# Average pooling 2x2: the multiply by 0.25 moved from ScalarE to VectorE, and the last tile split in 16, 8, 8

## The chip, the cores and the metric

The kernel runs on one core of a Trainium2 chip. The metric is device time in microseconds (us), as a median of several executions; lower is better. The profile shows the "span" of one execution, about 1.8 us shorter than its device time.

## The reference

```python
# x: float32 [32, 128, 256, 256], kernel_size = 2, stride = 2
for i in range(h_out):
    for j in range(w_out):
        window = x[:, :, 2*i:2*i+2, 2*j:2*j+2]
        output[:, :, i, j] = np.mean(window, axis=(2, 3))
```

1073.7 MB are read and 268.4 MB are written: each output is the sum of four inputs, times 0.25.

## The kernel before

An output row and its two input rows are one "row" of work; 128 rows, one per partition, are one unit, and there are 4096 units. A tile is 32 units: 64 KB of input and 16 KB of output per partition, 8.39 MB and 2.10 MB in all. There are 127 whole tiles (0 to 126) and a last one that is split in parts. Two input buffers and two result buffers alternate (a third result buffer serves the last tile alone). SyncE issues the loads, VectorE adds, ScalarE multiplies and issues the stores.

```python
    def sums(it, dst):                       # VectorE
        dve.tensor_add(out=it[:, :, 0:w], in0=it[:, :, 0:w], in1=it[:, :, w:]).then_inc(halfway)
        take(dve, halfway)                   # take = wait for a semaphore, then count it down
        dve.tensor_add(out=dst, in0=it[:, :, 0:w:2], in1=it[:, :, 1:w:2]).then_inc(summed)

    def tile_sums(b):
        take(dve, stored[b], 16)             # the store of two tiles ago has landed
        take(dve, loaded[b], 16)             # the load has landed
        sums(ins[b], res[b])

    def scale_store(t, b, landed):           # ScalarE
        take(act, summed)
        act.sem_inc(free[b])                 # SyncE may issue the load of tile t + 2
        scale(res[b])                        # act.mul(..., mul=0.25)
        take(act, scaled)
        act.dma_start(out=ot[t], in_=res[b]).then_inc(landed, 16)
    # ... SyncE: wait for free[b], load(t, b); then the parts of the last tile
    # ... parts of the last tile: 16, 8, 4, 4 units
    # ... the store of tile 126 is issued by SyncE, the parts' stores by ScalarE
```

Of the kernel before, what the change touches and what calls it, by code (L numbers as in the profile page):

```python
# [9 lines left out]
@with_exitstack  # L10
def kernel(
    ctx: ExitStack,
    tc: tile.TileContext,
    x: bass.AP,
    kernel_size: bass.AP,
    stride: bass.AP,
    out: bass.AP,
):
    nc = tc.nc
    P = nc.NUM_PARTITIONS  # L20

    n, c, h, w = x.shape
    k = int(kernel_size)
    s = int(stride)
    h_out = (h - k) // s + 1
    w_out = (w - k) // s + 1
    R = n * c * h_out
    units = R // P if R % P == 0 else 0


    if k == 2 and s == 2 and h % 2 == 0 and w == 256 and units >= 1024:
        _pool_2x2(ctx, tc, x, out, units)
    else:
        _generic_pool(ctx, tc, x, out, k, s, n, c, h, w, h_out, w_out)
# [5 lines left out]
def _pool_2x2(ctx, tc, x, out, units):  # L40
    nc = tc.nc
    P = nc.NUM_PARTITIONS
    f32 = mybir.dt.float32
    w = x.shape[3]
    w_out = w // 2
    sp, act, dve = nc.sync, nc.scalar, nc.vector

    xv = x.rearrange("n c (ho a) w -> (n c ho) (a w)", a=2)
    ov = out.rearrange("n c ho wo -> (n c ho) wo")


    in_pool = ctx.enter_context(tc.tile_pool(name="inp", bufs=2))
    out_pool = ctx.enter_context(tc.tile_pool(name="outp", bufs=3))
    ins = [in_pool.tile([P, TILE, 2 * w], f32, name="in_tile") for _ in range(2)]
    res = [out_pool.tile([P, TILE, w_out], f32, name="res") for _ in range(3)]

    def sem(name):
        return ctx.enter_context(nc.semaphore(name))

    loaded, free, stored = [[sem(f"{n}{b}") for b in range(2)] for n in ("loaded", "free", "stored")]  # L60
    halfway, summed, scaled, held, tail = [sem(n) for n in ("halfway", "summed", "scaled", "held", "tail")]



    def take(engine, sem, n=1):
        engine.wait_ge(sem, n)
        engine.sem_inc(sem, -n)  # L67

    def block(r0, g):
        rows = slice(r0, r0 + g * P)  # L70
        return xv[rows].rearrange("(p g) f -> p g f", p=P), ov[rows].rearrange("(p g) f -> p g f", p=P)

    whole, rest = divmod(units - 1, TILE)
    rest += 1
    xt = xv[0:whole * TILE * P].rearrange("(t p g) f -> t p g f", p=P, g=TILE)
    ot = ov[0:whole * TILE * P].rearrange("(t p g) f -> t p g f", p=P, g=TILE)
    parts, a = [], 0
    while a < rest:
        b = rest if rest - a <= 4 else a + (rest - a) // 2
        parts.append((a, b, sem(f"part{len(parts)}")))  # L80
        a = b

    def load(t, b):
        sp.dma_start(out=ins[b], in_=xt[t]).then_inc(loaded[b], 16)

    def sums(it, dst):
        dve.tensor_add(out=it[:, :, 0:w], in0=it[:, :, 0:w], in1=it[:, :, w:]).then_inc(halfway)  # L87
        take(dve, halfway)
        dve.tensor_add(out=dst, in0=it[:, :, 0:w:2], in1=it[:, :, 1:w:2]).then_inc(summed)  # L89

    def tile_sums(b):
        take(dve, stored[b], 16)
        take(dve, loaded[b], 16)
        sums(ins[b], res[b])

    def scale(dst, done=scaled):
        act.mul(out=dst, in_=dst, mul=0.25).then_inc(done)  # L97

    def scale_store(t, b, landed):
        take(act, summed)  # L100
        act.sem_inc(free[b])
        scale(res[b])
        take(act, scaled)
        act.dma_start(out=ot[t], in_=res[b]).then_inc(landed, 16)

    with tc.tile_critical():

        load(0, 0)
        load(1, 1)
        pairs = (whole - 2) // 2  # L110
        with sp.Fori(2, 2 + 2 * pairs, 2) as i:
            for b in range(2):
                take(sp, free[b])
                load(i + b, b)
        for t in range(2 + 2 * pairs, whole):
            take(sp, free[t % 2])
            load(t, t % 2)



        take(sp, free[whole % 2])
        it, dst = ins[whole % 2], res[2]
        for a, b, part in parts:
            sp.dma_start(out=it[:, a:b], in_=block((whole * TILE + a) * P, b - a)[0]).then_inc(part, 16)
        take(sp, held)
        sp.dma_start(out=ot[whole - 1], in_=res[(whole - 1) % 2]).then_inc(tail, 16)


        for b in range(2):
            dve.sem_inc(stored[b], 16)  # L130
        with dve.Fori(0, whole // 2):
            for b in range(2):
                tile_sums(b)
        if whole % 2:
            tile_sums(0)
        for a, b, part in parts:
            take(dve, part, 16)
            sums(it[:, a:b], dst[:, a:b])


        scale_store(0, 0, stored[0])
        pairs = (whole - 3) // 2
        with act.Fori(1, 1 + 2 * pairs, 2) as i:
            for b in (1, 0):
                scale_store(i + 1 - b, b, stored[b])
        for t in range(1 + 2 * pairs, whole - 1):
            scale_store(t, t % 2, stored[t % 2] if t < whole - 2 else tail)
        take(act, summed)
        scale(res[(whole - 1) % 2], held)
        for a, b, _ in parts:  # L150
            take(act, summed)
            scale(dst[:, a:b])
            take(act, scaled)
            act.dma_start(out=block((whole * TILE + a) * P, b - a)[1], in_=dst[:, a:b]).then_inc(tail, 16)


        take(sp, tail, 16 * (len(parts) + 2))
# [95 lines left out]
```

## Time and profile before

| | before |
|---|---|
| device time, median of 3 | 3103.32 us |
| VectorE busy / ScalarE busy | 54% / 15% |
| data moved, mean rate | 1342.2 MB, 433 GB/s |
| time from one tile to the next | 24.19 us |

From the page of the kernel before: the span, the busy time of each engine, the DMA row (each digit is the busy share of one fortieth of the span, in tenths), and the two DMA queues, q1 of the loads and q10 of the stores, with their share of the 16 DMA engines' time.

```profile
span 3101.5 us, 2614 instructions
DVE 1679.6 (54%) x262; ACT 464.7 (15%) x132; POOL 0.2 (0%) x4
...
DMA  9999999999999999999999999999999999999999
...
DMA packets 37728, 1342.19 MB, mean 433 GB/s; under 512 B 4192, under 2 KB 4192, under 8 KB 4576
...
q1 hardware_dynamic: 19008, 1075.85, 80.1%
q10 hardware_dynamic: 18720, 266.35, 20.1%
```

The two queues' shares add up to all of the engines' time: the DMA engines are full until shortly before the end, and nothing else is. The Trainium skill, "SBUF — State Buffer", section "SBUF: two separate sides", gives about 436 GB/s as what the DMA side of SBUF can carry; this trace agrees with 433.

The timeline of the kernel before in mid-run (start, duration, engine, line, operation; in brackets the idle time of the engine before it and what ended it):

```profile
1012.79 8.69 DVE L87 TENSOR_TENSOR in_tile<-in_tile 128x8192 f32<-128x8192 f32 x1 [10.93 <-DVEq L67]
1021.63 4.42 DVE L89 TENSOR_TENSOR res<-in_tile 128x4096 f32<-128x4096 f32 x1
1026.24 3.62 ACT L97 ACTIVATE res<-res 128x4096 f32<-128x4096 f32 x1 [20.58 <-ACTq L67]
1030.09 0.34 ACTq L104 DMA_DIRECT2D out_dram<-res  x1
1037.01 8.69 DVE L87 TENSOR_TENSOR in_tile<-in_tile 128x8192 f32<-128x8192 f32 x1 [10.95 <-DVEq L67]
```

VectorE waits 10.9 us in each tile. L67 is the wait for a semaphore; both a store's and a load's landing are waited for there. The DMA issues of the same kernel (count, size where known, median us from issue to landing):

```profile
out_dram<-res ACTq DMA_DIRECT2D x126, 2048.0 KB, 30.8
...
in_tile<-in_x_dram SPq DMA_DIRECT2D x127, 31.5
```

With a tile starting at T, its store is issued at T+17.3 and lands near T+48.1, just ahead of the start of the tile that uses the same buffers, at T+48.4. The load for that tile was issued at T+13.6 and landed near T+45.1. So in the kernel before VectorE is released by the store of two tiles ago; the load has been there for 3.27 us (median over the tiles, from the trace's landing records).

The end of the kernel before:

```profile
3067.57 8.69 DVE L87 TENSOR_TENSOR in_tile<-in_tile 128x8192 f32<-128x8192 f32 x1 [9.71 <-DVEq L67]
3076.41 4.43 DVE L89 TENSOR_TENSOR res<-in_tile 128x4096 f32<-128x4096 f32 x1
3080.75 4.42 DVE L87 TENSOR_TENSOR in_tile<-in_tile 128x4096 f32<-128x4096 f32 x1
...
3094.44 0.69 DVE L89 TENSOR_TENSOR res<-in_tile 128x512 f32<-128x512 f32 x1
3095.25 0.63 ACT L97 ACTIVATE res<-res 128x512 f32<-128x512 f32 x1 [1.34 <-ACTq L67]
3095.98 0.34 ACTq L154 DMA_DIRECT2D out_dram<-res  x1
```

Only here does VectorE work without a gap: from the start of tile 126 at 3067.57 its chain leads to the last store at 3095.98. That store in the DMA issues of the last microseconds, with its time to landing:

```profile
out_dram<-res ACTq DMA_DIRECT2D x1, 256.0 KB, 4.4
```

### The profile page before, as it was taken

To read this page: it belongs to the slowest core of one execution; us is meant where nothing else is said; L and a number is where in the kernel's file an instruction comes from. 1 tells how busy PE (TensorE), PEld (TensorE's weight loads), DVE (VectorE), ACT (ScalarE), POOL (GpSimd) and SP (SyncE) were. 2 spreads that over 40 slices of the span, in tenths; PEclk is the share of its full clock that TensorE was granted. 3 is DMA by queue.
4 is the path that set the end of the run, shared out by engine and by line. 5 is a ranking of instruction groups with operands and counts; after the bars stand their busy time and mean duration, and the time that the engine had idled before them with its cause. 6 is when DMAs were issued, how large, how long until landed. Compare 5 with 4: busy or idle time off the path is not lost. (4 is left out here: it accounts for less than half of the span.)

```text
span 3101.5 us, 2614 instructions
## 1 busy us (share of the span) xinstructions
DVE 1679.6 (54%) x262; ACT 464.7 (15%) x132; POOL 0.2 (0%) x4
## 2 busy tenths in 40 slices
DVE  4555555555555555555555555555555555555556
ACT  1111111111111111111111111111111111111111
POOL 0000000000000000000000000000000000000000
DMA  9999999999999999999999999999999999999999
GB/s 416 436 440 426 436 440 426 437 440 424 438 440 423 439 437 425 440 428 434 440 433 430 442 423 436 439 427 440 435 426 437 439 427 436 438 424 439 437 425 416
DMA packets 37728, 1342.19 MB, mean 433 GB/s; under 512 B 4192, under 2 KB 4192, under 8 KB 4576
## 3 DMA queue, kind: packets, MB, share of 16 engines
q1 hardware_dynamic: 19008, 1075.85, 80.1%
q10 hardware_dynamic: 18720, 266.35, 20.1%
HBM read 1073.74 MB, written 268.44 MB: 433 GB/s over the span
## 5 line engine op out<-in xcount | busy, mean ns | idle before, releaser
L87 DVE TENSOR_TENSOR in_tile<-in_tile 128x8192 f32<-128x8192 f32 (+1 forms) x131 | 1113.0, 8496 | 1396.4 <-DVEq L67 1396.4
L97 ACT ACTIVATE res<-res 128x4096 f32<-128x4096 f32 (+1 forms) x131 | 463.5, 3538 | 2594.8 <-ACTq L67 2594.8
L89 DVE TENSOR_TENSOR res<-in_tile 128x4096 f32<-128x4096 f32 (+1 forms) x131 | 566.8, 4327 | 19.2
L97 ACT ACT_TABLE_LOAD x1 | 1.3, 1283 | 36.3 <-ACTq L67 36.3
L234 POOL MEMSET const-bfloat16-1.0<- 128x1 bf16 x1 | 0.1, 101 | 0.0
L234 POOL MEMSET const-uint8-127<- 128x1 uint8 x1 | 0.1, 101 | 0.0
L234 POOL MEMSET const-float32-0.0<- 128x1 f32 x1 | 0.1, 98 | 0.2 <-issue 0.2
L234 POOL MEMSET const-float32-1.0<- 128x1 f32 x1 | 0.1, 98 | 0.0
## 6 DMA issues: line engine op xcount, KB each, us to landing
out_dram<-res ACTq DMA_DIRECT2D x126, 2048.0 KB, 30.8
in_tile<-in_x_dram SPq DMA_DIRECT2D x1, 4096.0 KB, 22.0
in_tile<-in_x_dram SPq DMA_DIRECT2D x1, 2048.0 KB, 27.1
in_tile<-in_x_dram SPq DMA_DIRECT2D x2, 1024.0 KB, 30.0
out_dram<-res SPq DMA_DIRECT2D x1, 2048.0 KB, 11.7
in_tile<-in_x_dram SPq DMA_DIRECT2D x127, 31.5
out_dram<-res ACTq DMA_DIRECT2D x1, 1024.0 KB, 8.1
out_dram<-res ACTq DMA_DIRECT2D x1, 512.0 KB, 6.0
```

The costliest lines, as they stand in the source:

```text
L87: dve.tensor_add(out=it[:, :, 0:w], in0=it[:, :, 0:w], in1=it[:, :, w:]).then_inc(halfway)
L89: dve.tensor_add(out=dst, in0=it[:, :, 0:w:2], in1=it[:, :, 1:w:2]).then_inc(summed)
L97: act.mul(out=dst, in_=dst, mul=0.25).then_inc(done)
L234: nc = _bacc.Bacc("TRN2", target_bir_lowering=False, num_devices=1)
```

## The change

The intent: let VectorE, which is idle 46% of the time, do the scaling in place, so that a tile has one hop between engines less before its store, and use fewer parts at the end. The diff, without renamings and loops, and without tile 126, whose store now waits for VectorE's multiply instead of ScalarE's:

```diff
-        b = rest if rest - a <= 4 else a + (rest - a) // 2      # 16, 8, 4, 4
+        b = rest if rest - a <= 8 else a + (rest - a) // 2      # 16, 8, 8
 ...
-        dve.tensor_add(out=dst, in0=it[:, :, 0:w:2], in1=it[:, :, 1:w:2]).then_inc(summed)
+        dve.tensor_add(out=dst, in0=it[:, :, 0:w:2], in1=it[:, :, 1:w:2]).then_inc(halfway)
+        take(dve, halfway)
+        dve.tensor_scalar_mul(out=dst, in0=dst, scalar1=0.25).then_inc(done)
 ...
-    def scale_store(t, b, landed):
-        take(act, summed)
+    def store(t, b, landed):
+        take(act, ready)
         act.sem_inc(free[b])
-        scale(res[b])
-        take(act, scaled)
         act.dma_start(out=ot[t], in_=res[b]).then_inc(landed, 16)
 ...
         for a, b, _ in parts:
-            take(act, summed)
-            scale(dst[:, a:b])
-            take(act, scaled)
+            take(act, ready)
             act.dma_start(...)
```

One side effect: the slot (the tile's input buffer) is now freed after the multiply, not before it, so the next load is issued later in the tile.

More of the change, by code (lines that the diff above doesn't have):

```diff
@@ L60, in _pool_2x2 @@
     loaded, free, stored = [[sem(f"{n}{b}") for b in range(2)] for n in ("loaded", "free", "stored")]
-    halfway, summed, scaled, held, tail = [sem(n) for n in ("halfway", "summed", "scaled", "held", "tail")]
+    halfway, ready, held, tail = [sem(n) for n in ("halfway", "ready", "held", "tail")]
     def take(engine, sem, n=1):
@@ L84, in load, with means, tile_means @@
         sp.dma_start(out=ins[b], in_=xt[t]).then_inc(loaded[b], 16)
-    def sums(it, dst):
+    def means(it, dst, done):
         dve.tensor_add(out=it[:, :, 0:w], in0=it[:, :, 0:w], in1=it[:, :, w:]).then_inc(halfway)
         take(dve, halfway)
-        dve.tensor_add(out=dst, in0=it[:, :, 0:w:2], in1=it[:, :, 1:w:2]).then_inc(summed)
-    def tile_sums(b):
+        dve.tensor_add(out=dst, in0=it[:, :, 0:w:2], in1=it[:, :, 1:w:2]).then_inc(halfway)
+        take(dve, halfway)
+        dve.tensor_scalar_mul(out=dst, in0=dst, scalar1=0.25).then_inc(done)
+    def tile_means(b, done):
         take(dve, stored[b], 16)
         take(dve, loaded[b], 16)
-        sums(ins[b], res[b])
-    def scale(dst, done=scaled):
-        act.mul(out=dst, in_=dst, mul=0.25).then_inc(done)
-    def scale_store(t, b, landed):
-        take(act, summed)
+        means(ins[b], res[b], done)
+    def store(t, b, landed):
+        take(act, ready)
         act.sem_inc(free[b])
-        scale(res[b])
-        take(act, scaled)
         act.dma_start(out=ot[t], in_=res[b]).then_inc(landed, 16)
@@ L130, in _pool_2x2 @@
             dve.sem_inc(stored[b], 16)
-        with dve.Fori(0, whole // 2):
+        pairs = (whole - 1) // 2
+        with dve.Fori(0, pairs):
             for b in range(2):
-                tile_sums(b)
-        if whole % 2:
-            tile_sums(0)
+                tile_means(b, ready)
+        for t in range(2 * pairs, whole):
+            tile_means(t % 2, ready if t < whole - 1 else held)
         for a, b, part in parts:
             take(dve, part, 16)
-            sums(it[:, a:b], dst[:, a:b])
-        scale_store(0, 0, stored[0])
-        pairs = (whole - 3) // 2
-        with act.Fori(1, 1 + 2 * pairs, 2) as i:
-            for b in (1, 0):
-                scale_store(i + 1 - b, b, stored[b])
-        for t in range(1 + 2 * pairs, whole - 1):
-            scale_store(t, t % 2, stored[t % 2] if t < whole - 2 else tail)
-        take(act, summed)
-        scale(res[(whole - 1) % 2], held)
+            means(it[:, a:b], dst[:, a:b], ready)
+        pairs = (whole - 2) // 2
+        with act.Fori(0, 2 * pairs, 2) as i:
+            for b in range(2):
+                store(i + b, b, stored[b])
+        for t in range(2 * pairs, whole - 1):
+            store(t, t % 2, stored[t % 2] if t < whole - 2 else tail)
         for a, b, _ in parts:
-            take(act, summed)
-            scale(dst[:, a:b])
-            take(act, scaled)
+            take(act, ready)
             act.dma_start(out=block((whole * TILE + a) * P, b - a)[1], in_=dst[:, a:b]).then_inc(tail, 16)
```

## The prediction

> **What bounds it now.** Data movement. The page's first table has VectorE busy 54% and ScalarE 15% of 3101.5 us, while the DMA row is at nine tenths or more in all 40 slices and moves 433 GB/s. 1342.2 MB at that rate is the whole span. The Trainium skill, "SBUF — State Buffer", section "SBUF: two separate sides", gives the DMA side of SBUF ~436 GB/s; this trace agrees (433).
>
> In the timeline a whole tile recurs every 24.19 us (8.39 MB in, 2.10 MB out). In it VectorE works 8.69 + 4.43 us and waits 10.9 us for a DMA landing; ScalarE works 3.62 us. By the table of DMA issues, loads land 31.5 us and stores 30.8 us after issue. With a tile starting at T, its load for two tiles on is issued at T+13.6 and lands near T+45; its store is issued at T+17.3 and lands near T+48.1; the next use of both buffers starts at T+48.4. So the store's landing, not the load's, releases VectorE. Both queues nevertheless always hold a waiting transfer, so the DMA engines don't run dry.
>
> **What the change does, per tile.** It removes a 3.62 us ScalarE activation and adds a VectorE multiply by a constant over 128x4096 f32. The trace has no such operation. The Trainium skill, "VectorE: DVE Perf Modes", section "The perf-mode tier table", has f32 SBUF scalar operations at twice the rate of a two-tensor operation; as an estimate it then costs what the trace's two-tensor add of half the elements costs: 2.29 us for 4096 elements, 1.22 for 2048, 0.69 for 1024. (At full length 4.43; no run here shows yet which.) VectorE goes to 15.6 us of 24.2. The slot comes free, and the next load is issued, about 2.4 us later in the tile (T+16); the store about 1.5 us earlier (T+15.8). Both only change how long a transfer queues: loads about 29 us from issue to landing, stores about 32. Nothing of it is on the path: the period stays 24.19 us.
>
> **The end.** There VectorE is the path. In the timeline it is busy without a gap from 3067.57 (sums of tile 126) to 3095.13; the last store (256 KB) is issued at 3095.98, lands 4.4 us later, and the span ends 1.1 us after that. With three multiplies more in front of the last store, two fewer parts' overheads, and a last part twice as large, I count, from the same 3067.57: tile 126 done 3083.3, the 16-unit part 3091.4, the first 8-unit part 3095.9, the second 3100.3; store issued 3100.5, landing in about 5 us (512 KB), end 3106.6: 5 us later than before. The DMA engines, full until about 3098 before, would idle in the last microseconds. If the multiply runs at one element per cycle, it is 9 to 10 us later.
>
> **Prediction.** 3108 us, 8 in 10 between 3101 and 3116. Faster by over 2%: 0.005; within 2%: 0.985; slower by over 2%: 0.01.
>
> **What would show each step.** Multiply 128x4096 near 2.3 us in the groups by form; VectorE's share about 63%; ScalarE 0; starts of successive tiles 24.19 us apart in mid-run; load landing down to about 29 us and store landing up to about 32; last store issued near 3100 with VectorE gapless before it.
>
> **What would make it wrong.** The order of loads and stores on the shared engines changes (loads later, stores earlier) and with it the rate: 0.3% of the rate is 9 us, as much as the whole tail. Parts landing later than VectorE wants them, since their issue is 2.4 us later. Tile 126 starting earlier because its buffer's store was issued earlier.

## The result, and the profile after

| | before | after |
|---|---|---|
| device time, median of 6 | 3103.57 us | 3105.77 us |
| VectorE / ScalarE busy | 54% / 15% | 64% / 0 |
| period in mid-run | 24.188 us | 24.186 us |
| start of tile 126 | 3067.57 | 3066.72 |
| last store issued / landed | 3095.98 / 3100.4 | 3099.50 / 3102.1 |
| span of the profiled run | 3101.5 | 3103.2 |

The ratio after to before is 1.0006, 95% interval 0.9993 to 1.0019: the same. A ratio is the mean time of one kernel's fast runs over that of the other's in the same rounds, so not quite the ratio of the medians in the table.

From the page of the kernel after:

```profile
span 3103.2 us, 2604 instructions
DVE 1973.3 (64%) x390; POOL 0.2 (0%) x4
...
DMA  9999999999999999999999999999999999999999
...
DMA packets 37440, 1342.19 MB, mean 433 GB/s; under 512 B 4160, under 2 KB 4160, under 8 KB 4416
```

The multiply at two sizes, from the groups by form (count, then busy us and mean ns of one):

```profile
L91 DVE TENSOR_SCALAR res<-res 128x4096 f32<-128x4096 f32 x127 | 291.4, 2294 | 18.9
...
L91 DVE TENSOR_SCALAR res<-res 128x2048 f32<-128x2048 f32 x1 | 1.2, 1227 | 0.1
```

It runs at about twice the rate of the two-tensor add (2294 against 4425 ns for the same 4096 elements), as the Trainium skill, "VectorE: DVE Perf Modes", section "The perf-mode tier table", has it: its figure for 2048 f32 elements is 1227 ns, and this trace has 1227.

The timeline of the kernel after in mid-run, and its DMA issues:

```profile
1010.77 8.69 DVE L87 TENSOR_TENSOR in_tile<-in_tile 128x8192 f32<-128x8192 f32 x1 [8.47 <-DVEq L67]
1019.61 4.42 DVE L89 TENSOR_TENSOR res<-in_tile 128x4096 f32<-128x4096 f32 x1
1024.18 2.29 DVE L91 TENSOR_SCALAR res<-res 128x4096 f32<-128x4096 f32 x1
1034.94 8.69 DVE L87 TENSOR_TENSOR in_tile<-in_tile 128x8192 f32<-128x8192 f32 x1 [8.47 <-DVEq L67]
```

```profile
out_dram<-res ACTq DMA_DIRECT2D x126, 2048.0 KB, 32.1
...
in_tile<-in_x_dram SPq DMA_DIRECT2D x127, 31.9
```

The distance of the starts is unchanged, 24.17 here. The multiply was taken out of VectorE's wait, which fell from 10.9 to 8.5 us. One thing differs from what I foresaw: loads take 31.9 us from issue to landing, not 29. Load and store of a pair are now issued at the same moment (T+16.06 and T+16.02) and land at the same moment: the load is there only 0.44 us before the tile starts, where it was 3.27 us in the kernel before.

The end of the kernel after, and its last store among the DMA issues:

```profile
3066.72 8.69 DVE L87 TENSOR_TENSOR in_tile<-in_tile 128x8192 f32<-128x8192 f32 x1 [8.47 <-DVEq L67]
3075.56 4.42 DVE L89 TENSOR_TENSOR res<-in_tile 128x4096 f32<-128x4096 f32 x1
3080.13 2.29 DVE L91 TENSOR_SCALAR res<-res 128x4096 f32<-128x4096 f32 x1
...
3098.70 0.69 DVE L91 TENSOR_SCALAR res<-res 128x1024 f32<-128x1024 f32 x1
```

```profile
out_dram<-res ACTq DMA_DIRECT2D x1, 512.0 KB, 2.6
```

The busy time in stretches of 2 us at the end, before first and then after (columns: stretch, its length, busy us of VectorE, [ScalarE,] GpSimd, clock, DMA share, GB/s):

```profile
3096.00:3098.00 2.00, 0.00 (x0) 0.00 (x0) 0.00 (x0) 1.00 0.96 388
3098.00:3100.00 2.00, 0.00 (x0) 0.00 (x0) 0.00 (x0) 1.00 0.47 181
```

```profile
3096.00:3098.00 2.00, 1.85 (x2) 0.00 (x0) 1.00 0.75 305
3098.00:3100.00 2.00, 1.25 (x2) 0.00 (x0) 1.00 0.03 10
3100.00:3102.00 2.00, 0.00 (x0) 0.00 (x0) 1.00 0.65 262
```

After, the DMA engines move almost nothing from 3098 to 3100 us: VectorE works on the last part until 3099.39, the last store is issued at 3099.50, and its first packet moves at 3100.35. That is where the kernel after loses time. From the start of tile 126 to the end of the span it needs 3103.2 - 3066.7 = 36.5 us, the kernel before 3101.5 - 3067.6 = 33.9. The end is 2.6 us longer, tile 126 starts 0.85 us sooner, and 2.6 - 0.85 is the 1.7 us by which the spans differ.

### The profile page after: what moved, and what is told of

It is laid out like the page before. It is cut to its first block, busy times and chain, and to the rows that moved or that the text cites. A ratio compares the mean times of both kernels' runs of the same rounds, so it can differ in the third digit from the quotient of the medians.

```text
span 3103.2 us, 2604 instructions
## 1 busy us (share of the span) xinstructions
DVE 1973.3 (64%) x390; POOL 0.2 (0%) x4
## 5 line engine op out<-in xcount | busy, mean ns | idle before, releaser
L91 DVE TENSOR_SCALAR res<-res 128x4096 f32<-128x4096 f32 (+1 forms) x130 | 294.0, 2261 | 19.4
## 6 DMA issues: line engine op xcount, KB each, us to landing
out_dram<-res ACTq DMA_DIRECT2D x126, 2048.0 KB, 32.1
out_dram<-res SPq DMA_DIRECT2D x1, 2048.0 KB, 13.6
in_tile<-in_x_dram SPq DMA_DIRECT2D x127, 31.9
```

The source lines that it names most:

```text
L91: dve.tensor_scalar_mul(out=dst, in0=dst, scalar1=0.25).then_inc(done)
```

## The experiments

My theory: the DMA engines set the pace in mid-run and hide everything that VectorE and ScalarE do there; what is left of the change is a longer chain at the end. Rivals: the coarser split costs the 2 us; or something in mid-run (the order of loads and stores) costs it; or VectorE is nearer to the path than its busy share tells. A run counts as slow when it is over 1.5% above the fastest of its kernel; all runs below are fast unless noted. The groups ran on different chips, so times are compared within a group, against the kernel before in the same rounds; profiles are one run each.

**Data movement alone (moves_only).** One small addition per tile in place of all arithmetic, the waits for loads and stores kept (and the result buffers set to 0 once at the start); the result is wrong.

```diff
-        ...     # two additions and the multiply over the tile, with the waits between them
+        dve.tensor_add(out=dst[:, :, 0:1], in0=it[:, :, 0:1], in1=it[:, :, w:w + 1]).then_inc(done)
```

> Same loads, stores, waits and split as the kernel after, with one small addition per tile in place of two additions and a multiply (result wrong on purpose). If the DMA engines bound the program: 1342.2 MB at 433.6 GB/s plus about 2 us before the first packet and 2 to 3 us after the last: 3100 to 3102 us, period 24.19 us. If VectorE's chain were what sets the pace, the tile would shrink by up to the 16 us that VectorE no longer works and the time would fall by several per cent.

Measured: 3103.59 us, ratio to before 0.9999 (0.9982 to 1.0016), period 24.18 us, VectorE busy 40 us in the whole run. Two successive tiles in mid-run:

```profile
1016.52 0.23 DVE L87 TENSOR_TENSOR res<-in_tile 128x32 f32<-128x32 f32 x1 [23.95 <-DVEq L67]
...
1040.69 0.23 DVE L87 TENSOR_TENSOR res<-in_tile 128x32 f32<-128x32 f32 x1 [23.94 <-DVEq L67]
```

Without its arithmetic the program is no faster than the kernel before, so in mid-run nothing that VectorE or ScalarE does is on the path. I had expected 3100 to 3102: here the stores run ahead and the parts of the last tile land late (the last at 3094.5, against 3090.5 in the kernel before), so this run is not a floor for the end.

**The multiply done two, three and four times (mul_x2, mul_x3, mul_x4).**

```diff
-        dve.tensor_scalar_mul(out=dst, in0=dst, scalar1=0.25).then_inc(done)
+        dve.tensor_scalar_mul(out=dst, in0=dst, scalar1=0.5).then_inc(halfway)
+        take(dve, halfway)
+        dve.tensor_scalar_mul(out=dst, in0=dst, scalar1=0.5).then_inc(done)    # and more, by 1.0
```

> Kernel after with two multiplies by 0.5. Off the path in mid-run, on it at the end: period 24.19 us, and the tail longer by 2.44 (tile 126) + 1.37 + 2 x 0.84 = 5.5 us, so about 3110 to 3112 us. If the multiply were on the path in every tile: 127 x 2.44 = 310 us more, about 3415 us.

> Three multiplies, VectorE 20.5 us busy of 24.19. The next load is issued at T+21 and the load before it ends at T+23.8[...]. Margin theory: period still 24.19 us, tail +11 us, 3115 to 3119 us. If the margin is smaller than I think, the period grows and the time is over 3130.

> Four multiplies, VectorE 22.7 us busy of 24.19, so by busy share it would still be hidden: 3105.8 + 16.5 = 3122 us. Margin theory: the load is issued at T+23.4 and finds its queue empty; two periods = 23.4 + 2 + 24.2 + 0.4 = 50.0 us, period 25.0 us, 3180 to 3250 us. This tells whether it is VectorE's idle time or the time from a tile's start to the next load's issue that must fit.

| | time, us | period, us | VectorE busy per tile | reserve, us | 64 KB packet, mean us |
|---|---|---|---|---|---|
| after | 3105.77 | 24.19 | 15.4 | 6.9 | 2.418 |
| mul_x2 | 3111.37 | 24.18 | 17.7 | 4.8 | 2.418 |
| mul_x3 | 3260.79 | 25.36 | 20.0 | 1.9 | 2.546 |
| mul_x4 | 3298.85 | 25.7 | 22.3 | 0.6 | 2.520 |

"Reserve" is the median time from the issue of a load to the landing, on the first of the 16 DMA engines to get there, of the load ahead of it: how long before it is needed the next load is in the queue. It and the packets' durations (those that start between 200 and 2900 us) are from the trace's landing and packet records. The ratios to before are 1.0025 (1.0008 to 1.0041), 1.0503 (1.0485 to 1.0521) and 1.0619 (1.0599 to 1.0639); before was at 3103.70 in these rounds. The 2 us in the sum for mul_x4 is an estimate of the time from a load's issue to its first packet in an empty queue; for the first load of the kernel before it was 1.0 us on the first of the 16 engines and 1.8 on the last.

mul_x2 came out as expected: 2.44 us more per tile cost nothing in 126 tiles, and from the start of tile 126 to the end of the span it needs 42.2 us instead of 36.5, which is 5.7 more. mul_x3 did not: I expected 3117 and got 3261, with VectorE still idle in a fifth of its time. From its page:

```profile
span 3262.1 us, 3124 instructions
DVE 2561.0 (79%) x650; POOL 0.2 (0%) x4
...
DMA  9999999999999999999999999999999999999997
...
DMA packets 37441, 1342.20 MB, mean 411 GB/s; under 512 B 4160, under 2 KB 4160, under 8 KB 4416
```

The DMA row is at nine tenths as before, but the rate is 411 instead of 433 GB/s. My mechanism, a queue that runs empty, does not show in mul_x3: fewer than 16 packets are in flight for only 2% of the time. Instead the 64 KB load packets themselves take longer, 2.546 us in the mean instead of 2.418, and of those over 2.6 us 83% start within 10 us after a load's issue (in the kernel after, none between tiles 5 and 120 is over 2.6). Eight load and eight store packets per engine make a tile's transfer, and 8 x (2.546 + 0.621) = 25.34 us is close to the measured period, 25.36; in the kernel before 8 x (2.418 + 0.611) = 24.23. Why load packets are slow shortly after an issue that comes late, no run here tells; nor was mul_x3 run with its slots freed before the multiplies, which would tell the late issue from VectorE's longer work in this kernel itself. In mul_x4, above the 3180 to 3250 us that I had expected, there is idle time too (4% of the time with fewer than 16 packets in flight). So mul_x3 and mul_x4 show that time is lost before VectorE is busy for the whole period, but not by the mechanism that I had given for it.

**The split alone, and the place of the scaling at the end alone (after_again, after_split4, before_split8, tail_on_act), on one chip in the same rounds.** after_again is the kernel after; after_split4 and before_split8 exchange the one number in the split; tail_on_act is the kernel after, but ScalarE scales tile 126 and the last tile's parts:

```diff
-            tile_means(t % 2, ready if t < whole - 1 else held)
+            tile_means(t % 2, ready, t < whole - 1)             # tile 126: two additions only
 ...
-            means(it[:, a:b], dst[:, a:b], ready)
+            means(it[:, a:b], dst[:, a:b], ready, False)
 ...
+        take(act, ready)
+        act.mul(out=res[(whole - 1) % 2], in_=res[(whole - 1) % 2], mul=0.25).then_inc(held)
         for a, b, _ in parts:
             take(act, ready)
+            act.mul(out=dst[:, a:b], in_=dst[:, a:b], mul=0.25).then_inc(scaled)
+            take(act, scaled)
```

> The kernel after unchanged, as the control of this group: 3105 to 3106.5 us, ratio to before 1.0005 to 1.001.

> Kernel after with the last tile in 16, 8, 4, 4 units as before. VectorE's end chain gets one more part's three fixed overheads (last store issued 0.8 us later), the last store is half as large and lands about 0.6 us sooner: 3105.6 to 3106.4 us, the same as after within 0.5. If the coarser split were the cause of the 2 us, this returns to 3103.5.

> Kernel before with the last tile in 16, 8, 8 units. The DMA engines are full nearly to the end there, last store issued 0.1 to 0.2 us later but twice as large: 3103.5 to 3104.3 us. If the split were the cause of the 2 us, this goes to 3105.5.

> Kernel after (VectorE multiplies tiles 0 to 125, split 16, 8, 8), but tile 126 and the last tile are scaled by ScalarE as before. If the multiplies in VectorE's end chain cost the 2 us, this comes back to 3102.8 to 3104.0 us. If something in the 126 tiles of mid-run (order of loads and stores) costs it, this stays at 3105.5 to 3106.

| | median, us | ratio to before (95%) | start of tile 126 | end of span minus that |
|---|---|---|---|---|
| before (same rounds) | 3103.51 | | (3067.57) | (33.9) |
| before_split8 | 3103.20 | 0.9999 (0.9986 to 1.0013) | 3067.75 | 33.8 |
| after_again | 3103.96 | 1.0004 (0.9990 to 1.0018) | 3065.72 | 36.5 |
| after_split4 | 3105.19 | 1.0004 (0.9991 to 1.0018) | 3066.72 | 36.6 |
| tail_on_act | 3102.49 | 0.9998 (0.9984 to 1.0012) | 3065.83 | 34.7 |

(In brackets: from the profile of before that was shown above.) By time alone all five are the same, and the control itself came back to 3103.96 (its five runs go from 3103.78 to 3107.32), so the times that I had set for tail_on_act decide nothing. By the last column the split costs nothing in either kernel (33.9 and 33.8; 36.5 and 36.6). after_again and tail_on_act start tile 126 within 0.1 us of each other and differ in nothing but who scales at the end: 36.5 against 34.7. The start of tile 126 in after_again, then in the timeline of tail_on_act the same, the first part, the last part and the last store:

```profile
3065.72 8.69 DVE L87 TENSOR_TENSOR in_tile<-in_tile 128x8192 f32<-128x8192 f32 x1 [8.46 <-DVEq L67]
```

```profile
3065.83 8.69 DVE L87 TENSOR_TENSOR in_tile<-in_tile 128x8192 f32<-128x8192 f32 x1 [8.47 <-DVEq L67]
...
3080.09 4.43 DVE L87 TENSOR_TENSOR in_tile<-in_tile 128x4096 f32<-128x4096 f32 x1 [0.99 <-DVEq L67]
...
3092.88 1.22 DVE L89 TENSOR_TENSOR res<-in_tile 128x1024 f32<-128x1024 f32 x1
3094.22 1.06 ACT L153 ACTIVATE res<-res 128x1024 f32<-128x1024 f32 x1 [2.52 <-ACTq L67]
3095.39 0.34 ACTq L155 DMA_DIRECT2D out_dram<-res  x1
```

The last store leaves at 3095.39 instead of 3098.51 in after_again, and lands 4.1 us later instead of 2.6, because the DMA engines are still full then. So 3.1 us of VectorE's chain are worth 1.7. The chain isn't gapless there: VectorE waits 0.99 us for the load of the first part, which lands at 3079.95. In the kernel before it lands at 3080.03, in time, since tile 126 starts 1.7 us later there; the wait is about what its end is shorter by (33.9 instead of 34.7). An earlier start of tile 126 is thus in part lost to waiting for data. after_again came out 1.0 us under the lower end that I had given (the other three by 0.3 to 0.4 us): tile 126 started 1.0 us sooner than in the first profile of the same kernel; in that profile the 16 DMA engines landed a load up to 1.3 us apart at the end of the run, in after_again 0.45, and the last of them counts.

**What sets the distance between the landings of a load and of its store (first_store_late, free_early, late_free_early).** I had expected loads to land in 29 us in the kernel after and it was 31.9. The packet records don't name the DMA engine, but they show sixteen 64 KB load packets and sixteen 16 KB store packets in turn, which I read as one of each per engine (the Trainium skill, "DMA: Bandwidth & Descriptors", section "Queues, rings and completion order", says that an engine goes round its queues packet by packet; this trace agrees, 2.418 and 0.611 us). Eight of each make a tile. So a lag of the stores behind the loads, once made, should stay. In the kernel before store 0 was issued at 41.36 us and its first packets went at 46.7, behind two packets of load 2 on each engine; in the kernel after at 39.10 and 44.1, behind one. first_store_late delays the first store alone; free_early frees all slots early; late_free_early does both.

```diff
 # first_store_late, tile 0 only:
+            dve.sem_inc(free[0])
+            dve.tensor_scalar_mul(out=dst, in0=dst, scalar1=1.0).then_inc(halfway)
+            take(dve, halfway)
         dve.tensor_scalar_mul(out=dst, in0=dst, scalar1=0.25).then_inc(done)
 # free_early, every tile that has a load to release:
         take(dve, halfway)
+        dve.sem_inc(free[slot])             # and no longer by ScalarE, after the multiply
         dve.tensor_scalar_mul(out=dst, in0=dst, scalar1=0.25).then_inc(done)
```

> Kernel after, but tile 0 alone is multiplied twice (by 1.0, then 0.25) and its input slot is freed before that: load 2 issued near 36.7 us and store 0 near 41.5 us, as in the kernel before; all later tiles as in the kernel after. If the distance between the landings of a load and of the store that goes with it is set once, at the start, by which packets the two queues pair: the store lands about 3.0 us (one 64 KB plus one 16 KB packet) after its load in the whole run, loads land about 29 us after issue and stores 32. If it follows from when each tile issues them, it stays at 0.2 us, 31.9 and 32.1. Time within 1.5 us of after under both.

> Kernel after, but VectorE frees the input slot itself after the second addition, so each load is issued at T+13.5 instead of T+16.1, and the first store when it was. Theory of the start: the landings stay 0.2 us apart, loads 34.4 us from issue to landing, stores 32.1. Theory of the issue order: landings about 3 us apart, loads 31.5. Time the same as after within 1 us: an earlier issue only queues longer.

> first_store_late and free_early together: the first store is late, so each store should land about 3 us after its load in the whole run (VectorE starts 3.27 us after its load has landed), but every load is issued at T+13.6 as in the kernel before. If first_store_late was slow in three of four runs because the load's issue came too late (on the first DMA engine to finish, only about 2.5 us before the load ahead of it ended there), the reserve is back at about 5 us or more, all runs are at 3103 to 3106 us, period 24.19 us, loads 31.5 us from issue to landing. If the late first store is itself what makes it slow, runs of 3170 us and more come again.

| | store 0 issued | load issued in mid-run | store lands after its load by | reserve | time, us |
|---|---|---|---|---|---|
| before | 41.36 | T+13.6 | 3.02 | 6.3 | 3103.57 |
| after | 39.10 | T+16.1 | 0.19 | 6.8 | 3105.77 |
| free_early | 39.08 | T+13.6 | 0.17 | 9.7 | 3104.01 |
| late_free_early | 41.38 | T+13.6 | 3.02 | 6.6 | 3105.97 |
| first_store_late | 41.38 | T+16.0 | 3.02 | 2.5 | 3176 to 3185, once 3105.4 |

The theory of the start holds in all three (first_store_late's profile is of a slow run): the lag is 3.02 us, about one packet pair, where two packets of load 2 went ahead of the first store, and 0.2 where one did, whatever the later tiles do. The clock time of the first store is not what counts: mul_x2 issued it at 41.52, later than the kernel before, but its load 2 came late too (41.58), one packet went ahead, and the lag is 0.17. The DMA issues of free_early show the other half of it, that an earlier issue only queues longer:

```profile
out_dram<-res ACTq DMA_DIRECT2D x126, 2048.0 KB, 32.1
...
in_tile<-in_x_dram SPq DMA_DIRECT2D x127, 34.3
```

I had not expected first_store_late to be slow, in three of four runs (3176.12, 3179.91, 3185.27 and 3105.40; the kernel before was at 3102.7 to 3104.3 in the same rounds). The profiled run is one of the slow ones and shows the picture of mul_x3, without more work for VectorE: 423 GB/s, a period of 24.77 us, 64 KB packets of 2.489 us in the mean, loads that land in 30.1 us and stores in 33.2, and a reserve of 2.5 us. late_free_early keeps the late first store and gives the reserve back: four runs of 3105.8 to 3106.9 (I had allowed up to 3106), and loads that land in 31.5 us as foretold. So the late first store alone did not make it slow. That it does so together with the later issue of every load fits, but is not shown: it rests on four runs of each, on two chips (three of four slow against none of four). Every kernel profiled here with a reserve of 4.8 us or more holds 24.19 us; the three with 2.5 us or less do not, first_store_late in three of four runs. I build nothing else on the slow runs.

free_early was also 1.8 us under the first measurement of the kernel after, where I had allowed 1 (but level with after_again, 3103.96), and late_free_early was not. They have the same end chain, and from the start of tile 126 to the end of the span both need 36.5 us, as the kernel after does; the times are 3104.01 and 3105.97, which is 0.6 and 2.5 over before in their own rounds. Tile 126 starts at 3065.47 and 3067.55. The store of tile 124, which it waits for, lands on the first of the 16 DMA engines at 3064.85 and 3066.25, and on the last one 0.4 and 1.1 us later: so of the 2.1 us, 1.4 go with the lag, and 0.7 with how far the engines are apart. The end chain hangs on the start of tile 126, and this on the lag made at the start of the program and on that spread.

**A version to beat both (best).** tail_on_act with the split 16, 8, 4, 4 and a fourth result buffer for tile 126:

```diff
-    res = [out_pool.tile([P, TILE, w_out], f32, name="res") for _ in range(3)]
+    res = [out_pool.tile([P, TILE, w_out], f32, name="res") for _ in range(4)]
 ...
-        take(dve, stored[b], 16)
+        if scaled_here:                      # not for tile 126
+            take(dve, stored[b], 16)
```

> tail_on_act with the split 16, 8, 4, 4 and a buffer of its own for the result of tile 126, so that it needn't wait for the store of tile 124: VectorE's end chain starts at the landing of load 126 (about 0.2 us sooner than in after). 3102.5 to 3103.8 us; within 1 us of before, since the DMA engines are then full to within 3 us of the end.

Measured: 3102.46 us, ratio to before 0.9997 (0.9983 to 1.0011). It is the lowest median with tail_on_act (3102.49), about 1 us under before, and no gain that the interval can tell from none. The DMA engines are full to within 3 us of the end; an earlier last store only lands more slowly. The result's own buffer did start VectorE sooner (its wait before tile 126 is 8.19 us instead of 8.47 in tail_on_act), but the time went into the wait for the first part's load, 1.28 us instead of 0.99.

## Why the prediction was right or wrong

- **Right: the range.** 3105.77 us, foretold 3108 (3101 to 3116), within 2%. This alone says little: the kernel before, at 3103.57, lies in the same range, and the size, 5 us foretold, came out at 2.2 here and at 0.45 in after_again, neither of which the intervals tell from none. The steps below are what was tested.
- **Right: the bound.** Period 24.19 us before and after, and the program without arithmetic takes the same time (moves_only).
- **Right: the multiply.** 2.29 us foretold, 2.294 measured; VectorE 64% of the span against "about 63%"; stores 32.1 us to landing against "about 32".
- **Right: VectorE's chain is the path at the end**, shown by mul_x2 (5.7 us longer from the start of tile 126, expected 5.5) and by tail_on_act (1.8 us shorter).
- **Mis-sized: "landing in about 5 us (512 KB)".** The last store landed in 2.62 us. I took the 4.4 us of the kernel before, where the DMA engines were still full, though the same paragraph says that they would idle now. That is 2.4 of the 3.4 us by which the end was foretold too late (3106.6 against 3103.2).
- **Mis-sized: "from the same 3067.57".** Tile 126 started at 3066.72; the remaining 0.15 us lies in the hop to the store's issue. The list of what would make the prediction wrong had it ("Tile 126 starting earlier because its buffer's store was issued earlier"). The cause that the runs show is narrower: not each tile's earlier store (late_free_early has that too and starts tile 126 at 3067.55), but the first store's place behind one packet of load 2 instead of two. That this start came 0.85 us sooner in the profiled run was in part luck: in after_again, the same kernel, it is 1.85.
- **Wrong: "Both only change how long a transfer queues: loads about 29 us".** Loads took 31.9. I let the later issue shorten the queueing and kept the 3 us between the landings. Those 3 us were made at the start of the program and went when the first store came behind one load packet instead of two; first_store_late, free_early and late_free_early show it. It cost no time in mid-run.

Where the expected gain of the change went: nowhere, since ScalarE's 3.6 us and the hop were never on the path in mid-run. At the end, where VectorE's chain is the path, the change lengthened it, and an earlier start of tile 126 and an idle DMA gave part of that back.

What stays open: why load packets take longer shortly after an issue that comes late; and what spreads the 16 DMA engines' landings by 0.4 us in one run and 1.3 in another. With that spread the start of tile 126 moved by 1.0 us between two profiles of the kernel after. What made one run of after_again 3107.32 us, 3.3 over the next, is not known either; it was not profiled.

## What to carry to other kernels

When the DMA engines are full, and the next load is issued early enough (4.8 us or more ahead was enough here), moving arithmetic between engines changed the time only at the two ends: at the end of the program, where the DMA engines run dry, and through what its start sets up. So cost it there, from the start of the last chain to the last store's landing, and take a landing time from a moment in which the DMA engines are as loaded as they will be. An engine's idle share is not its margin: here VectorE was idle in a fifth of mul_x3 and the program had lost 5%; what went with the loss in these runs was how long before its turn the next load is issued. A full DMA row doesn't prove full rate: read the GB/s beside it.

## What the Trainium skill lacked or had wrong

- "DMA: Bandwidth & Descriptors" has nothing on load packets that take longer when the next load is issued only shortly before its turn: 2.546 us in the mean instead of 2.418 per 64 KB (mul_x3, reserve 1.9 us; not seen at 4.8 us or more).
- The same page's "Queues, rings and completion order" has the turn-taking right, but not what follows for two queues that are both always waiting: a lag of about one packet pair, 3.02 us, made by the first store's place lasted through the run. It also describes a packet as typically 9 to 17 descriptors; the packets recorded in these traces are one partition's contiguous 64 or 16 KB, and the queues change after each. How many descriptors such a record holds, the profile doesn't tell.
- The same page's "Anatomy of one DMA — SWDGE (gpsimd) path" fits 2.0 us plus bytes at 436 GB/s, for DMAs issued by GpSimd, which gives an estimate of 3.2 us for 512 KB; the last store of the kernel after, issued by ScalarE with the DMA engines otherwise idle, landed in 2.62 us, that of after_split4 (256 KB) in 2.02, and one of 1024 KB in mul_x3 in 3.85. These three give, as an estimate, about 1.4 us plus the bytes at 433 GB/s. The page's fit is for another path, so this does not show it wrong.
